# The cached past's key tile among the first token tiles, and the first head's q and k transposed inside the projection stage

## The chip, the cores and the metric

The kernel runs on one core of a Trainium2 chip. The core has five engines that each execute their own list of instructions in order: TensorE (PE), VectorE (DVE), ScalarE (ACT), GpSimd (POOL) and SyncE (SP, which here only issues transfers). The metric is the device time of one execution in microseconds; lower is better.

## The reference

One step of a hybrid encoder layer over 1024 prompt tokens and 64 decode tokens; the decode tokens also see 128 cached positions. What matters here is latent attention with 8 heads: q and kv are projected down to 256 columns, normalised, and projected up; each head's q and k are normalised too.

```python
q = (rmsnorm(c_q, g_cq) @ w_uq).reshape(B, S, N_HEADS, QK_DIM)        # 256 -> 8 x 96
lat_new = rmsnorm(c_kv, g_ckv)                                        # 256 columns
lat_all = lat_new if past_lat is None else jnp.concatenate([past_lat, lat_new], axis=1)
kv = (lat_all @ w_ukv).reshape(B, T, N_HEADS, QK_NOPE + V_DIM)        # 256 -> 8 x (64 + 64)
k_nope = rmsnorm(kv[..., :QK_NOPE], g_kn)
v = kv[..., QK_NOPE:]
```

Ahead of it stands the normalisation and the input projection, behind it softmax over a block-causal mask, the output maps with sigmoid gates, a mixture of 32 experts, and an embedding term. None of that is touched.

## The kernel before

The program runs in stages: the input projection (0 to 282 us of the span), the projections of q and kv from their latents (282 to 407, here called the projection stage), eight heads of attention (407 to 690), the output maps, the router, the experts (897 to 1225) and a tail. A product in f32 is made of two or three matmuls of a high and a low half (`h` and `l` in a tile's name): `mm3` writes them at lines 62 to 64, `mm2` at lines 68 and 69. `hi` casts a high half on ACT (line 56), `lo` takes the rest on DVE (line 59).

The projection stage is a loop over i from 0 to NT + 2, with NT = 9 token tiles. `L_mm(i)` makes the 544 latent columns of tile i on PE (24 matmuls of 256 columns and 24 of 288), `L_stat` and `L_norm` normalise them, `L_tr` transposes them on PE (five transposes), `L_ev` evicts and splits them. Three tiles behind follow `q_a` and `kv_a` (matmuls of 384 and of 512 columns, statistics, and V, which is written to DRAM as `vd`) and `q_b` and `kv_b` (scaling, and writes of q and k to DRAM as `qnd` and `knd`). `qnd` is held in pieces of 4, 4 and 1 tiles, `knd` in pieces of 4, 4 and 2. Tile 9 of k and v belongs to the cached past: its latents come from the input (`pl`), `L_past` splits them, and `kv_a(9)`, `kv_b(9)` make k and v from them, with a `fold` of the two halves by a copy on ACT (line 442) and an add on DVE (line 443). The weights of k and v, `wukv0` and `wukv1`, arrive one after the other through one staging tile, `wup_r`, ahead of the loop, and are split by a cast on ACT and a subtraction on DVE.

From i = NT on, `fill_n(4)` puts gate matmuls (24 of 384 or of 320 columns for a piece) into the stage; they need only `hT` and weights `fw` that POOL's queue loads. All of the stage's PSUM tiles come from `bank()`, a pool of eight. For a head, `kq_load` reloads q and k of two heads into `qs_` and `ks_` on SP's queue (a reload waits for the writes of its piece), `prep_k` and `prep_q` transpose them on PE and split them into kT and qT; S, softmax and PV follow, with more gate matmuls (`fg`) between them.

A scheduler sets the order of each engine's list from the program and its own model; each engine then executes its list strictly in that order, so an instruction that waits holds up all behind it on the same engine. At the end of the stage the code before reads:

```python
    kv_a(9)
    kv_b(9)
    fill_n(4)
    psA.close()
...
    kq_load(0)
    v_load(0)
    v_load(1)
    for f in preps(0):
```

Of the kernel before, what the change touches and what calls it, by code (L numbers as in the profile page):

```python
# [7 lines left out]
F32 = mybir.dt.float32  # L8
# [3 lines left out]
AF = mybir.ActivationFunctionType  # L12
OP = mybir.AluOpType
# [3 lines left out]
T = 1088  # L17
NP = 1024
NS = 64
NT = 9  # L20
# [3 lines left out]
NK = 1216  # L24
# [15 lines left out]
def body(ctx, tc, a):  # L40
    nc = tc.nc
# [9 lines left out]
    def opened(*args, **kw):  # L51
        st = ExitStack()
        return st, st.enter_context(pool(*args, **kw))

    def hi(dst, src):
        nc.scalar.copy(dst, src)  # L56

    def lo(dst, src, h, eng=None):
        (eng or nc.vector).tensor_tensor(out=dst, in0=src, in1=h.bitcast(F32), op=OP.subtract)  # L59

    def mm3(ps, sh, sl, mh, ml, first, last):
        r = nc.tensor.matmul(ps, sh, mh, start=first, stop=False)  # L62
        nc.tensor.matmul(ps, sh, ml, start=False, stop=False)  # L63
        nc.tensor.matmul(ps, sl, mh, start=False, stop=last)  # L64
        return r

    def mm2(ps, st, mh, ml, first, last):
        nc.tensor.matmul(ps, st, mh, start=first, stop=False)  # L68
        nc.tensor.matmul(ps, st, ml, start=False, stop=last)  # L69
# [13 lines left out]
    def rstd(out, ss, scale, n):  # L83
        nc.gpsimd.tensor_scalar(out=out, in0=ss, scalar1=scale, scalar2=EPS, op0=OP.mult, op1=OP.add)
        nc.gpsimd.tensor_tensor(out=out, in0=out, in1=mhalf[:out.shape[0], :n], op=OP.pow)
# [7 lines left out]
    ident = keep.tile([128, 128], F32, name="ident")  # L93
# [16 lines left out]
    def bank():  # L110
        return pb.tile([128, 512], F32, name="bk", tag="bk")
# [249 lines left out]
    for j, (kind, d, g) in enumerate(jobs):  # L361
        if kind == "a" and d == 0:
            open_gate()
        f = evs[kind](d)
# [6 lines left out]
        for ci, (o, n) in enumerate([c for c in CH if c[0] < TB] if kind in "ag" else CH):  # L371
            ps = bank()
# [41 lines left out]
    for src, dst in ((gkr, rk), (gqr, rq)):  # L414
        for half in range(2):
            for w in range(2):
                nc.vector.tensor_tensor(
                    out=dst[:, :, 32 * w + 16 * half:32 * w + 16 * half + 16],
                    in0=rope[:, :, 16 * w:16 * w + 16],
                    in1=src[:, None, 16 * half:16 * half + 16].to_broadcast([128, NT, 16]), op=OP.mult)  # L420
# [20 lines left out]
    def fold(ps, tmp):  # L441
        nc.scalar.copy(tmp[0:64], ps[64:128])
        nc.vector.tensor_tensor(out=ps[0:64], in0=ps[0:64], in1=tmp[0:64], op=OP.add)
# [56 lines left out]
    def L_past():  # L500
        th = lp.tile([128, 2, 128], F32R, name="latTh", bufs=2)
        hi(th[:, :, 0:64], pl[:, :, 64:128])
        lo(th[:, :, 64:128], pl[:, :, 64:128], th[:, :, 0:64])
        latT[9] = (th, None)
# [39 lines left out]
    def kv_a(i):  # L544
        xh, xl = latT.pop(i)
        kn = hwp.tile([128, NH, 64], F32, name="kn")
        V = hwp.tile([128, NH, 128], F32R, name="V", bufs=1)
        p2 = [bank(), bank()]
        for b in range(2):
            for k in range(2):  # L550
                wh, wl = (x[:, 512 * b:512 * b + 512] for x in wk[k])
                if i < 9:
                    mm3(p2[b], xh[:, k], xl[:, k], wh, wl, k == 0, k == 1)
                else:
                    mm2(p2[b], xh[:, k], wh, wl, k == 0, k == 1)
            if i == 9:
                fold(p2[b], kn.rearrange("p h c -> p (h c)"))
        nc.scalar.activation(kn.rearrange("p h c -> p (h c)"), p2[0], AF.Square)
        ss = hwp.tile([128, 8], F32, name="ssk")
        nc.vector.tensor_reduce(out=ss, in_=kn, axis=AX.X, op=OP.add)  # L560
        rs = hwp.tile([128, 8], F32, name="rsk")
        rstd(rs, ss, 1.0 / 64, 8)
        for par in range(2):
            src = p2[1].rearrange("p (j t c) -> p j t c", t=2, c=64)[:, :, par]
            vi = V.rearrange("p (j t) c -> p j t c", t=2)[:, :, par]
            vh = vi[:, :, 64 * par:64 * par + 64]
            hi(vh, src)
            lo(vi[:, :, 64 - 64 * par:128 - 64 * par], src, vh)
        nc.sync.dma_start(vd[:, :, i].rearrange("h p c -> p h c"), V.bitcast(F32))
        st4["k", i] = (p2[0], rs, kn)  # L570

    def kv_b(i):
        p, rs, kn = st4.pop(("k", i))
        nc.vector.tensor_tensor(out=kn, in0=p.rearrange("p (h c) -> p h c", h=8),
                                in1=rs[:, :, None].to_broadcast([128, NH, 64]), op=OP.mult)
        nc.sync.dma_start(knd[i // 4][:, :, i % 4].rearrange("q p c -> p q c"), kn.rearrange("p (q t) c -> p q (t c)", t=2))
# [43 lines left out]
    def fill_n(n):  # L620
        for _ in range(n):
            if fill:
                fill.pop(0)()
# [7 lines left out]
    hws, hwp = opened("hw", bufs=2, side="right")  # L631
    kq, vv = {}, {}

    def kq_load(p):
        qs_ = qk.tile([128, NT, 192], F32, name="qs_", bufs=1)
        ks_ = qk.tile([128, 10, 128], F32, name="ks_", bufs=1)
        for t in range(3):
            k1, q1 = min(10, 4 * t + 4), min(NT, 4 * t + 4)
            nc.sync.dma_start(ks_[:, 4 * t:k1], knd[t][p])
            nc.sync.dma_start(qs_[:, 4 * t:q1], qnd[t][p])  # L640
        kq[p] = (qs_, ks_)

    def v_load(h):
        vv[h] = qk.tile([128, 10, 128], F32R, name="vs_", bufs=2)
        nc.gpsimd.dma_start(vv[h], vd[h])

    for i in range(NT + 3):
        if i < NT:
            L_mm(i)
            L_stat(i)  # L650
        if i == NT - 1:
            gs_["q"].close()
            hs.close()
            fgs, fgp = opened("fgate", bufs=2)
            fg_load(0)
            qks, qk = opened("qk")
            kT = qk.tile([112, 4, NK], F32R, name="kT")
            qT = qk.tile([112, 4, T], F32R, name="qT")
            kTh, kTl, qTh, qTl = ([x[:, s + j] for j in range(2)] for x in (kT, qT) for s in (0, 2))
            qg = qk.tile([96, 1], F32, name="qg")  # L660
            nc.vector.tensor_copy(qg, qgain)
            nc.gpsimd.dma_start(kT[96:112], a["kmask"])
            nc.gpsimd.dma_start(qT[96:112], a["qmask"])
        if 1 <= i <= NT:
            L_norm(i - 1)
        if 2 <= i <= NT + 1:
            L_tr(i - 2)
            L_ev(i - 2)
        if i == NT + 1:
            L_past()  # L670
            for j in range(2):
                nc.scalar.copy(kTh[j][64:96, :], kpe)
                lo(kTl[j][64:96, :], kpe, kTh[j][64:96, :])
        if i >= 3:
            q_a(i - 3)
            kv_a(i - 3)
            q_b(i - 3)
            kv_b(i - 3)
        if i >= NT:
            fill_n(4)  # L680
    kv_a(9)
    kv_b(9)
    fill_n(4)
    psA.close()

# [9 lines left out]
    pT = psS.enter_context(pool("psT", bufs=2, space=PSUM))  # L695
    pO = psS.enter_context(pool("psO", bufs=1, space=PSUM))
    psF.append(psS.enter_context(pool("psF", bufs=1, space=PSUM)))
    def prep_k(h, t0):
        par = h % 2
        kn = kq[h // 2][1]  # L700
        nt = min(4, 10 - t0)
        ps = pT.tile([128, 512], F32, name="tp")
        for t in range(nt):
            nc.tensor.transpose(ps[0:64, 128 * t:128 * t + 128], kn[:, t0 + t, 64 * par:64 * par + 64], ident)
        c = 128 * t0
        n = min(128 * nt, NK - c)
        hi(kTh[par][0:64, c:c + n], ps[0:64, :n])
        lo(kTl[par][0:64, c:c + n], ps[0:64, :n], kTh[par][0:64, c:c + n])

    def prep_q(h, t0):  # L710
        par = h % 2
        qn = kq[h // 2][0]
        nt = min(4, NT - t0)
        ps = pT.tile([128, 512], F32, name="tp")
        for t in range(nt):
            nc.tensor.transpose(ps[0:96, 128 * t:128 * t + 128], qn[:, t0 + t, 96 * par:96 * par + 96], ident)
        c = 128 * t0
        n = min(128 * nt, T - c)
        nc.scalar.activation(qTh[par][0:96, c:c + n], ps[0:96, 0:n], AF.Copy, scale=qg)
        nc.vector.scalar_tensor_tensor(out=qTl[par][0:96, c:c + n], in0=ps[0:96, 0:n], scalar=qg,  # L720
                                       in1=qTh[par][0:96, c:c + n].bitcast(F32), op0=OP.mult, op1=OP.subtract)

    def preps(h):
        return [lambda t0=t0, f=f: f(h, t0) for t0 in (0, 4, 8) for f in (prep_k, prep_q)]

    UN = []
    for h in range(NH):
        for p in (3, 0, 2, 1) if h else (0, 1, 2, 3):
# [100 lines left out]
        nc.vector.tensor_tensor(out=aT[j][g, c0:c0 + n], in0=tmp[g, :n], in1=po[g, :n], op=OP.add)  # L829

    todo = []
    kq_load(0)
    v_load(0)
    v_load(1)
    for f in preps(0):
        f()
# [142 lines left out]
    for d in range(8):  # L979
        w = st6.pop(("w", d))  # L980
        for ci, (o, n) in enumerate(MCH):
            ps = bank()
# [195 lines left out]
    for i in range(6):  # L1178
        p = i - 1
# [345 lines left out]
    with tc.For_i(0, nov, 1) as i:  # L1525
# [7 lines left out]
        ps = bank()  # L1533
# [11 lines left out]
        for k in range(KD):  # L1545
# [4 lines left out]
            h, l = xT["o", k // 4]  # L1550
# [4 lines left out]
        h, l = aT2["o"]  # L1555
        pso = [bank(), bank()]
        for j in range(2):
            for b in range(2):
                c = slice(512 * b, 512 * b + 512)
# [224 lines left out]
```

## Time and profile before

| | |
|---|---|
| time, median of 3 runs | 1350.8 us (1348.19 to 1350.96) |
| profiled execution | 1351.81 us, its span 1349.8 us, mean granted clock 0.982 |
| PE busy | 1268.6 us, 94% of the span |
| DVE, ACT, POOL busy | 848.0, 649.7, 323.8 us |
| PE busy, 400 to 420 us | 14.26 us of 20, granted clock 0.83 |

The times in the rows are microseconds from the start of the span. A row of a timeline gives the start, the duration, the engine, the line of the kernel, the operation, the tile it writes and those it reads, and in brackets the engine's idle time just ahead of it and what ended that. The granted clock is a share of 2.4 GHz. Matmuls overlap in the engine, so the distance of two starts tells more than a duration.

### The profile page before, as it was taken

How to read it: one execution, taken by the hardware profiler on the slowest of the kernel's cores; microseconds unless marked ns; L12 is line 12 of the kernel's file. 1: busy time of each engine (PE TensorE's matmuls, PEld its weight loads, DVE VectorE, ACT ScalarE, POOL GpSimd, SP SyncE). 2: the span in 40 equal slices, each digit the busy share in tenths (PEclk: the TensorE clock that was granted, in tenths of full speed). 3: DMA queues.
4: the chain of work that ended last, by engine and by line, in shares of the span. 5: the costliest groups of instructions: out<-in, count | busy, mean ns of one | idle time of the engine just before them, and what ended most of it. 6: DMA issues, size and time to landing. Idle time of an engine off the chain costs nothing. (4 is left out here: it accounts for less than half of the span.)

```text
span 1349.8 us, 20413 instructions
## 1 busy us (share of the span) xinstructions
PE 1268.6 (94%) x7235; PEld 1100.1 (81%) x7235; DVE 848.0 (63%) x1627; ACT 649.7 (48%) x1276; POOL 323.8 (24%) x375
## 2 busy tenths in 40 slices
PE   7999999998998999999999999749999999999998
PEld 6999999998987988888998888537666666667886
DVE  6433243325675466666659755678988889884743
ACT  6212142223344455555545211338888888886322
POOL 2000001124663333333315200232222222210210
PEclk9999999999998999999999999869999999999999
DMA  5111298734477523242257656769999999967511
GB/s 197 64 34 45 78 355 299 276 117 137 138 188 223 176 69 125 86 150 73 82 197 265 247 201 225 252 185 350 364 346 346 340 345 347 346 235 272 204 39 55
DMA packets 106057, 272.36 MB, mean 202 GB/s; under 512 B 13521, under 2 KB 42689, under 8 KB 105922
## 3 DMA queue, kind: packets, MB, share of 16 engines
q1 hardware_dynamic: 89968, 220.29, 47.1%
q0 software_dynamic: 15840, 50.68, 11.7%
q8 instruction: 58, 0.95, 0.3%
q14 instruction: 45, 0.37, 0.1%
q10 hardware_dynamic: 146, 0.07, 0.0%
HBM read 211.14 MB, written 67.19 MB: 206 GB/s over the span
## 5 line engine op out<-in xcount | busy, mean ns | idle before, releaser
L59 DVE TENSOR_TENSOR wel<-eraw,weh 128x1024 fp32r<-128x1024 f32 x190 | 226.3, 1220 | 34.4 <-ACT weh L56 32.4
L56 ACT CAST weh<-eraw 128x1024 fp32r<-128x1024 f32 x192 | 196.0, 1054 | 11.7 <-PE bk L64 10.7
L769 POOL TENSOR_TENSOR P<-P,ri 128x128 f32<-128x128 f32 (+8 forms) x72 | 77.2, 1077 | 129.2 <-DVE ri L768 109.6
L63 PE MATMUL bk<-wel,xTh 128*96 128x512 f32 x256 | 103.5, 404 | 1.5 <-DVE wel L59 1.4
L62 PE MATMUL bk<-weh,xTh 128*96 128x512 f32 x256 | 102.5, 400 | 1.7 <-ACT xTh L56 1.7
L64 PE MATMUL bk<-weh,xTl 128*96 128x512 f32 x256 | 103.1, 403 | 0.0
L1337 POOL DMA_INDIRECT Yd<-y,idx x32 | 41.3, 1292 | 227.2 <-ACT y L1334 217.5
L59 DVE TENSOR_TENSOR wl<-w_r,wh 128x1024 fp32r<-128x1024 f32 x28 | 34.3, 1225 | 75.7 <-ACT wh L56 75.3
L62 PE MATMUL bk<-hTAh,wh 128*128 128x384 f32 x224 | 76.6, 342 | 1.8 <-ACT hTAh L56 1.8
L63 PE MATMUL bk<-hTAl,wh 128*128 128x384 f32 x224 | 76.4, 341 | 0.0
L64 PE MATMUL bk<-hTAh,wl 128*128 128x384 f32 x224 | 76.1, 340 | 0.0
L62 PE MATMUL fg<-hTBh,fw 128*128 128x384 f32 (+1 forms) x224 | 74.9, 334 | 0.3 <-ACT fgm L605 0.2
L56 ACT CAST wh<-w_r 128x1024 fp32r<-128x1024 f32 x28 | 29.4, 1050 | 91.8 <-PE bk L63 86.3
L64 PE MATMUL fg<-hTBh,fw 128*128 128x384 f32 (+1 forms) x224 | 73.3, 327 | 0.0
L63 PE MATMUL fg<-hTBl,fw 128*128 128x384 f32 (+1 forms) x224 | 73.1, 326 | 0.0
L62 PE MATMUL bk<-hTBh,wh 128*128 128x384 f32 (+1 forms) x192 | 62.2, 324 | 0.0
L63 PE MATMUL bk<-hTBl,wh 128*128 128x384 f32 (+1 forms) x192 | 62.0, 323 | 0.0
L64 PE MATMUL bk<-hTBh,wl 128*128 128x384 f32 (+1 forms) x192 | 61.8, 323 | 0.0
L63 PEld LDWEIGHTS bk<-wel,xTh 128*96 128x96 f32 x256 | 41.7, 163 | 22.2 <-DVE wel L59 7.8
L62 PE MATMUL bk<-weh,ath 128*96 128x512 f32 x128 | 50.9, 397 | 8.8 <-ACT ath L56 8.8
L755 DVE TENSOR_REDUCE nm<-S 128x1 f32<-128x128 f32 (+8 forms) x72 | 50.8, 706 | 12.7 <-PE S L64 11.6
L62 PEld LDWEIGHTS bk<-weh,xTh 128*96 128x96 f32 x256 | 41.6, 162 | 19.3 <-ACT xTh L56 3.3
(782 smaller groups left out, 3750.8 us busy)
## 6 DMA issues: line engine op xcount, KB each, us to landing
eraw<-in_we_dram SPq DMA_DIRECT2D x192, 512.0 KB
fw<-wsd POOLq DMA_DIRECT2D x32, 512.0 KB, 4.3
w_r<-in_wing_dram SPq DMA_DIRECT2D x28, 512.0 KB
gm_r<-gscr SPq DMA_DIRECT2D x16, 544.0 KB
wsd<-wh SPq DMA_DIRECT2D x16, 512.0 KB
wsd<-wl SPq DMA_DIRECT2D x16, 512.0 KB
xy<-Yd SPq DMA_DIRECT2D x16, 512.0 KB
vd<-V SPq DMA_DIRECT2D x10, 512.0 KB
```

What stands on the lines that cost most here:

```text
L56: nc.scalar.copy(dst, src)
L59: (eng or nc.vector).tensor_tensor(out=dst, in0=src, in1=h.bitcast(F32), op=OP.subtract)
L62: r = nc.tensor.matmul(ps, sh, mh, start=first, stop=False)
L63: nc.tensor.matmul(ps, sh, ml, start=False, stop=False)
L64: nc.tensor.matmul(ps, sl, mh, start=False, stop=last)
L755: nc.vector.tensor_reduce(out=nm, in_=s, axis=AX.XY, op=OP.max, negate=True)
L769: nc.gpsimd.tensor_tensor(out=P[:, :nk], in0=P[:, :nk], in1=ri.to_broadcast([128, nk]), op=OP.mult)
L1337: nc.gpsimd.indirect_dma_start(out=Yd[:, :], out_offset=bass.IndirectOffsetOnAxis(ap=col, axis=0), in_=buf, in_offset=None, bounds_check=A ...
```

## The change

`L_past()`, `kv_a(9)` and `kv_b(9)` move from the end of the loop to i = 2. `kq_load` takes a range of pieces; for the first two heads its first two pieces are put at i = NT + 1 and its third at i = NT + 2. `prep_k` and `prep_q` move up in the program and can take a bank of the stage's pool; for head 0 the first two pieces of both are transposed at i = NT + 2, ahead of the last gate fill, and `preps(0)` keeps only the third piece.

```diff
@@ -631,18 +631,46 @@
-    def kq_load(p):
-        qs_ = qk.tile([128, NT, 192], F32, name="qs_", bufs=1)
-        ks_ = qk.tile([128, 10, 128], F32, name="ks_", bufs=1)
-        for t in range(3):
+    def kq_load(p, ta=0, tb=3):
+        if ta == 0:
+            kq[p] = (qk.tile([128, NT, 192], F32, name="qs_", bufs=1), qk.tile([128, 10, 128], F32, name="ks_", bufs=1))
+        qs_, ks_ = kq[p]
+        for t in range(ta, tb):
             k1, q1 = min(10, 4 * t + 4), min(NT, 4 * t + 4)
             nc.sync.dma_start(ks_[:, 4 * t:k1], knd[t][p])
             nc.sync.dma_start(qs_[:, 4 * t:q1], qnd[t][p])
-        kq[p] = (qs_, ks_)
...
+    def prep_k(h, t0, get=None):
+        par = h % 2
+        kn = kq[h // 2][1]
+        nt = min(4, 10 - t0)
+        ps = get() if get else pT.tile([128, 512], F32, name="tp")
+        for t in range(nt):
+            nc.tensor.transpose(ps[0:64, 128 * t:128 * t + 128], kn[:, t0 + t, 64 * par:64 * par + 64], ident)
...
+    def preps(h):
+        return [lambda t0=t0, f=f: f(h, t0) for t0 in ((0, 4, 8) if h else (8,)) for f in (prep_k, prep_q)]
...
@@ -661,13 +689,16 @@
+        if i == 2:
+            L_past()
+            kv_a(9)
+            kv_b(9)
         if 1 <= i <= NT:
             L_norm(i - 1)
         if 2 <= i <= NT + 1:
             L_tr(i - 2)
             L_ev(i - 2)
         if i == NT + 1:
-            L_past()
             for j in range(2):
...
@@ -676,10 +707,15 @@
+        if i == NT + 1:
+            kq_load(0, 0, 2)
         if i >= NT:
             fill_n(4)
-    kv_a(9)
-    kv_b(9)
+        if i == NT + 2:
+            kq_load(0, 2, 3)
+            for t0 in (0, 4):
+                prep_k(0, t0, bank)
+                prep_q(0, t0, bank)
     fill_n(4)
     psA.close()
...
-    kq_load(0)
     v_load(0)
```

Where this puts instructions on PE, among the first tiles (`wukv` is the weight of k and v, `latTh` the past's latents, `ident` marks a transpose of `L_tr`, `wq` the matmuls of `L_mm`); lines with a plus are new there:

```order
 L64 MATMUL bk<-wq7h,hTAl 128x288
+L68 MATMUL bk<-wukv0h,latTh 128x512 x2
 L479 MATMUL bk<-ident,cq 128x128
 L480 MATMUL bk<-ident,ltk 128x128
...
 L63 MATMUL bk<-wq4l,hTBh 128x288
+L68 MATMUL bk<-wukv1h,latTh 128x512 x2
 L64 MATMUL bk<-wq4h,hTBl 128x288
...
 L64 MATMUL bk<-wq7h,hTBl 128x288
+L69 MATMUL bk<-wukv1l,latTh 128x512 x2
 L479 MATMUL bk<-ident,cq 128x128
```

The eight matmuls of the past's tile now stand in four pairs: the first behind `L_mm(2)`, one within `L_mm(3)` (not shown), one ten matmuls before the end of `L_mm(3)`, and one behind it.

PE at the end of the stage, before: behind the gate fill of 384 columns stand the matmuls of the past's tile, and only behind the fill of 320 columns the first transposes of q and k (`ks_`, `qs_`):

```order
L68 MATMUL bk<-wukv0h,latTh 128x512
...
L69 MATMUL bk<-wukv1l,latTh 128x512
L62 MATMUL bk<-hTBh,fw_3722 128x320
...
L64 MATMUL bk<-hTBh,fw_3723 128x320
L704 MATMUL tp<-ident,ks__4045 64x128 x4
L716 MATMUL tp<-ident,qs__4044 96x128 x4
L704 MATMUL tp<-ident,ks__4045 64x128 x4
L62 MATMUL S<-kT,qT 128x128
L63 MATMUL S<-kT,qT 128x128
```

and of the change:

```order
L64 MATMUL bk<-hTBh,fw_3755 128x384
L653 MATMUL bk<-ident,ks__3860 64x128 x4
L665 MATMUL bk<-ident,qs__3859 96x128 x4
L653 MATMUL bk<-ident,ks__3860 64x128 x4
L665 MATMUL bk<-ident,qs__3859 96x128 x4
L62 MATMUL bk<-hTBh,fw_3754 128x320
...
L64 MATMUL bk<-hTBh,fw_3755 128x320
L653 MATMUL tp<-ident,ks__3860 64x128 x2
L665 MATMUL tp<-ident,qs__3859 96x128
L62 MATMUL S<-kT,qT 128x128
L63 MATMUL S<-kT,qT 128x128
```

Two pieces of k and of q stand ahead of the fill of 320 columns, and the first S stands behind the third piece of both.

SP at the same place, before (`knd` and `qnd` are the pieces in DRAM, `kn` and `qn` what is written to them, `gscr` and `fy` belong to the gates):

```order
L640 DMA qs__4044<-qnd_65 128x768
L576 DMA knd_69<-kn 128x4x128
L611 DMA gscr<-fgm 128x384
L594 DMA fy<-ycd 128x320
L639 DMA ks__4045<-knd_68 128x512
L542 DMA qnd_66<-qn 128x4x192
L611 DMA gscr<-fgm 128x320
L594 DMA fy<-ycd 128x384
L569 DMA vd<-V 128x8x128
L576 DMA knd_69<-kn 128x4x128
L640 DMA qs__4044<-qnd_66 128x192
L639 DMA ks__4045<-knd_69 128x256
```

and of the change:

```order
L641 DMA qs__3859<-qnd_65 128x768
L576 DMA knd_69<-kn 128x4x128
L640 DMA ks__3860<-knd_68 128x512
L611 DMA gscr<-fgm 128x384
L594 DMA fy<-ycd 128x320
L640 DMA ks__3860<-knd_69 128x256
L542 DMA qnd_66<-qn 128x4x192
L641 DMA qs__3859<-qnd_66 128x192
```

The reload of the second piece of k moves ahead of the gates' transfers, that of the third piece ahead of the last q write, and the past's writes are gone from here.

## Rows read from the trace of the kernel before

**Rows 1.** Windows: busy time of each engine by stretch, clock, DMA share, GB/s.

```profile
core 0: us, PE busy (x) PEld busy (x) DVE busy (x) ACT busy (x) POOL busy (x), PEclk, DMA share, GB/s
320.00:400.00 80.00, 78.72 (x497) 74.04 (x496) 57.21 (x163) 31.64 (x100) 47.65 (x57) 1.00 0.52 144
400.00:420.00 20.00, 14.26 (x73) 13.26 (x72) 10.97 (x26) 5.24 (x11) 9.75 (x12) 0.83 0.96 295
430.00:690.00 260.00, 250.36 (x1696) 234.96 (x1695) 161.34 (x359) 140.85 (x361) 90.98 (x97) 1.00 0.34 109
```

**Rows 2.** Timeline of PE, 299 to 319: start, duration, line, operation, [idle before].

```profile
300.34 0.27 PE L479 MATMUL bk<-ident,cq 128*128 128x128 f32 x1
...
306.87 0.27 PE L479 MATMUL bk<-ident,cq 128*128 128x128 f32 x1
...
307.33 0.42 PE L62 MATMUL bk<-wuq0h,cqTh 128*128 128x384 f32 x1
...
313.83 0.72 PE L62 MATMUL bk<-wukv0h,latTh 128*128 128x512 f32 x1 [4.17 <-ACT qn L520]
...
318.26 0.28 PE L62 MATMUL bk<-wq0h,hTBh 128*128 128x256 f32 x1
```

**Rows 3.** Timeline of ACT, 298 to 320: the casts of the wukv weights.

```profile
300.96 1.05 ACT L56 CAST wukv0h<-wup_r 128x1024 fp32r<-128x1024 f32 x1 [4.72 <-DMA wup_r<-in_wukv_dram]
...
310.99 1.04 ACT L56 CAST wukv1h<-wup_r 128x1024 fp32r<-128x1024 f32 x1 [6.98 <-DMA wup_r<-in_wukv_dram]
```

**Rows 4.** Timeline of PE, 397 to 424: end of the projection stage, first head.

```profile
397.49 0.33 PE L62 MATMUL bk<-hTBh,fw 128*128 128x384 f32 x1
...
401.65 0.40 PE L68 MATMUL bk<-wukv0h,latTh 128*128 128x512 f32 x1
...
403.50 0.31 PE L62 MATMUL bk<-hTBh,fw 128*128 128x320 f32 x1
...
407.02 0.60 PE L704 MATMUL tp<-ident,ks__4045 128*64 128x128 f32 x4
...
413.97 1.06 PE L704 MATMUL tp<-ident,ks__4045 128*64 128x128 f32 x4 [4.81 <-DVE kT L59]
...
415.15 0.63 PE L62 MATMUL fg<-hTBh,fw 128*128 128x384 f32 x1
...
421.84 0.33 PE L64 MATMUL fg<-hTBh,fw 128*128 128x384 f32 x1
...
422.25 0.38 PE L704 MATMUL tp<-ident,ks__4045 128*64 128x128 f32 x2
...
423.39 0.44 PE L62 MATMUL S<-kT,qT 112*128 112x384 f32 x1 [0.63 <-ACT P L762]
```

**Rows 5.** Timeline of ACT, 399 to 420: first fold copy of the past's tile.

```profile
406.09 0.58 ACT L442 COPY kn<-bk 64x512 f32<-64x512 f32 x1 [3.75 <-DMA knd<-kn]
```

**Rows 6.** Timeline of DVE, 399 to 420: rest of the first k block.

```profile
413.24 0.67 DVE L59 TENSOR_TENSOR kT<-tp,kT 64x512 fp32r<-64x512 f32 x1
```

**Rows 7.** Timeline of POOL, 395 to 420: the last q tile's rsq.

```profile
402.76 2.90 POOL L90 TENSOR_TENSOR rsq<-rsq,mhalf 128x16 f32<-128x16 f32 x1
```

**Rows 8.** Timeline of SP, 395 to 420: issues of writes and reloads.

```profile
401.04 0.36 SPq L542 DMA_DIRECT2D qnd<-qn  x1
...
401.64 0.36 SPq L576 DMA_DIRECT2D knd<-kn  x1
...
403.80 0.33 SPq L640 DMA_DIRECT2D qs__4044<-qnd  x1
...
404.22 1.29 SPq L576 DMA_DIRECT2D knd<-kn  x1
...
410.82 0.37 SPq L542 DMA_DIRECT2D qnd<-qn  x1
...
415.68 0.33 SPq L640 DMA_DIRECT2D qs__4044<-qnd  x1
...
418.83 0.33 SPq L639 DMA_DIRECT2D ks__4045<-knd  x1
```

**Rows 9.** DMA issues, 395 to 425: KB each, median us to landing.

```profile
fw<-wsd POOLq DMA_DIRECT2D x4, 512.0 KB, 4.8
```

More of the change, by code (lines that the diff above doesn't have):

```diff
@@ L645, in v_load, with prep_q @@
         nc.gpsimd.dma_start(vv[h], vd[h])
+    def prep_k(h, t0, get=None):
[5 more added lines that the diff above has]
+            nc.tensor.transpose(ps[0:64, 128 * t:128 * t + 128], kn[:, t0 + t, 64 * par:64 * par + 64], ident)
+        c = 128 * t0
+        n = min(128 * nt, NK - c)
+        hi(kTh[par][0:64, c:c + n], ps[0:64, :n])
+        lo(kTl[par][0:64, c:c + n], ps[0:64, :n], kTh[par][0:64, c:c + n])
+    def prep_q(h, t0, get=None):
+        par = h % 2
+        qn = kq[h // 2][0]
+        nt = min(4, NT - t0)
+        ps = get() if get else pT.tile([128, 512], F32, name="tp")
+        for t in range(nt):
+            nc.tensor.transpose(ps[0:96, 128 * t:128 * t + 128], qn[:, t0 + t, 96 * par:96 * par + 96], ident)
+        c = 128 * t0
+        n = min(128 * nt, T - c)
+        nc.scalar.activation(qTh[par][0:96, c:c + n], ps[0:96, 0:n], AF.Copy, scale=qg)
+        nc.vector.scalar_tensor_tensor(out=qTl[par][0:96, c:c + n], in0=ps[0:96, 0:n], scalar=qg,
+                                       in1=qTh[par][0:96, c:c + n].bitcast(F32), op0=OP.mult, op1=OP.subtract)
+    def preps(h):
+        return [lambda t0=t0, f=f: f(h, t0) for t0 in ((0, 4, 8) if h else (8,)) for f in (prep_k, prep_q)]
     for i in range(NT + 3):
@@ L697, in body @@
     psF.append(psS.enter_context(pool("psF", bufs=1, space=PSUM)))
[L698 to L724, printed above, removed]
     UN = []
```

## The prediction

> **What bounds the kernel now.** I read the engines' busy shares by stretch first, then the timeline of PE around the two places that the diff touches, then the timelines of ACT, DVE, POOL and SP there, to see what ends PE's waits. PE sets the pace: from 320 to 400 us it is busy 78.72 of 80, and in the heads, from 430 to 690, 250.36 of 260 [rows 1]. An instruction put on PE there, or a wait of PE there, is therefore paid nearly in full. Between those two stretches lies the one visible hole: from 400 to 420 PE works 14.26 us of 20 and its granted clock is 0.83 [rows 1]. A second one lies at the start of the stage: PE stands 4.17 us before the matmul at 313.83 [rows 2]. The change works at both places.
>
> How the late hole comes about: the eight matmuls of the cached past's tile (I call them kv9) run from 401.65 to 403.50, the gate fill of 320 columns to 407.02, then the first four k transposes; the next k transposes start only at 413.97, after a wait that DVE's kT ended [rows 4]. That kT (413.24, [rows 6]) needs ACT's cast, and ACT came late because the fold copy of kv9 waited 3.75 us for the write of an older kn and began at 406.09 [rows 5]; all of kv9's copies and casts stood ahead of kT on ACT. After the wait the fill of 24 matmuls takes from 415.15 until its last one starts at 421.84, so 6.86 us to its end at about 422.0, against 4.16 for the same 24 from 397.49 to 401.65 [rows 4]: 2.7 us lost at the lower of the two clock levels (1.2 instead of 2.4 GHz). Wait and slow clock together are about 8.5 us, which the change aims at.
>
> **The early place.** kv9's matmuls now stand in the first token tiles, in four pairs. The first pair needs wukv0h, whose cast runs from 300.96 to 302.01 [rows 3]; PE gets there at 300.34 [rows 2] and so waits 1.7. L_tr(0) and L_mm(3) take 6.53 (300.34 to 306.87, [rows 2]); the third pair stands ten matmuls before their end, ten of 48 being some 1.3 us. A matmul of 512 columns costs 1.85 / 8 = 0.23 [rows 4]. So PE has 2 x 0.46 + 5.2 to do and is at the third pair at 302.0 + 6.1 = 308.2, but wukv1h is cast only from 310.99 to 312.03, when its weights have landed [rows 3]: a wait of 3.9. Those weights come by a transfer issued long before; nothing in the change moves it. What is left behind this wait: the third pair 0.46, ten matmuls 1.3, the fourth pair 0.46, L_tr(1) 0.46 (306.87 to 307.33), q_a(0) some 2.2 (from 307.33, with the 4.17 of idle before 313.83 taken off), and the twelve matmuls of kv_a(0), 12 x 0.23 = 2.8 [rows 2]. That is 7.7, to 319.7, against 318.26 before: +1.4 with a full clock throughout. Before, kv_a(0) after its wait of 4.17 took 4.43 (313.83 to 318.26) instead of 2.8, 1.65 lost to the lower clock [rows 2]. A wait of 3.9, with one of 1.7 just ahead, is nearest to that row, so I add 1.65: +3.1. If the clock stays low as long as in the late row, 2.7 instead of 1.65: +4.1. The range of this term is +1.4 to +4.1. The old wait of 4.17 is not a saving: it was the same wait for wukv1h, with ACT's work behind it, and it is now met with more work left over. kv9's own 1.85 is inside this term, since PE has no other idle time until 400.
>
> Also moved with it: the fold, square and casts on ACT and DVE and the writes of vd and knd on SP. In tile 0 ACT has idle time and PE has L_mm(4), some 6 us, to run meanwhile; I cost them at nothing, and take their exposure as a rival.
>
> **The late place**, in the clock time of the trace before, PE at 401.65 [rows 4]. kv9 is gone, so the first k and q transposes follow at once, 0.4 each (five took 0.46 at 306.87, [rows 2]): PE is done at 402.5. Next on PE, in front of the fill, stand the second k transposes, and they need the reload of the second key block. On SP this reload stands behind the knd write at 404.22, which took 1.29 to issue, and needs the write issued at 401.64 to be back [rows 8]. A write is back 2.8 (401.04 to 403.80) to 4.9 later (410.82 to 415.68) [rows 8]. So the issue falls at 405.5 to 406.5. The trace before shows no duration for this read. The reload issued at 418.83 was used at 422.25, so it took 3.4 at most [rows 4, 8]; 512 KB loads take 4.8 [rows 9]; I use 2.8 to 4.8, taking the shortest write as the floor. The block of 256 KB is then there at 408.3 to 411.3, and I take 409.8. **PE waits 7.3** (5.8 to 8.8), and the fill of 3.5 us (403.50 to 407.02) that covered such waits before is now queued behind the waiting transposes. Then k and q transposes 0.9, the fill 3.5 and, after a wait as long as that of 413.97, the same 2.7 of slow clock: 416.9 (415.4 to 418.4).
>
> Behind it on PE stand the last k and q transposes, which need the reload of the last q block. Its chain: the q write stands on SP behind the reload of the last k block, and that one waits for the knd write of 404.22 to come back, 407.0 to 409.1. Its data need rsq, which POOL has at 405.66 [rows 7], and seven short DVE operations, ready earlier than before, when the fold stood among them and the write was issued at 410.82 [rows 8]. So the issue is at 407.4 to 410.8; I take 409.0. With a write of 2.8 to 4.9 and a read of 2.8 to 4.8 the block lands at 413 to 420.5, middle 416.7. Both legs end together; S starts at about 417.4, three S matmuls take 0.4, the fill of 24 at full clock 4.16: 421.9, against 422.0 for the same point before. What before still had behind that point is saved: the last k transposes, 0.14 (422.25), and a wait of 0.63 in front of 423.39 [rows 4], since softmax starts earlier. **Late term: -0.9** (-2.5 to +2.6, from the ends of both chains).
>
> So the hole of 8.5 is not closed: kv9's tail is replaced by the way through DRAM and back, and the fill that hid part of that way now stands behind it.
>
> Here a rule can be set against the rows. What the rows show is 2.8 to 4.9 for one leg [rows 8]. The Trainium skill, "DMA: Bandwidth & Descriptors", section "Anatomy of one DMA", puts a transfer at some 2.0 us fixed plus the bytes over the rate. By it, as an estimate, the reload of 256 KB would take 2.6 and the write as long, and the sum would be that of the first rival. The rows of this stretch stand above it, with DMA busy 0.96 of the time [rows 1], so I go by them.
>
> **Sum.** +3.1 - 0.9 = +2.2 us. On the profiled execution (1351.81, its span 1349.8) that is 1354.0; it stands 1.0 over the median of the runs, so on 1350.8 I forecast **1353.0**. A measurement of this kernel can tell about 0.2% from no change, 2.7 us, and the forecast lies just within.
>
> **Rivals.**
> 1. Short legs: every write and read takes 2.8. Then the second key block lands at 408.3, PE is through the fill at 415.4 and the last q block lands at 413.0: late -2.5. With the early term at its middle the sum is +0.6, 1351.4. For it: the leg of 2.8 at 401.04. Against: the leg of 4.9 nine us later. Chance 0.2.
> 2. Faster, by the clock alone: PE keeps 2.4 GHz over both waits. Early +1.4; late, with 2.7 less in front of S, 416.9 becomes 414.2, but S still waits for the last q block, so this counts only if that one lands by then: late -0.9 - 3.2 = -4.1. Sum -2.7, 1348.1; the point that decides is S started by 414.2 with fill matmuls at 0.15 to 0.17 us each. Against it speak both waits of before, after each of which the clock fell. Chance 0.15 with versions still better.
> 3. Slower, early: V has one buffer, so V of tile 0 waits for the write of kv9's V, and ACT stands in order behind it. A write of 4.9 [rows 8] after the first cast, with ACT's queue behind it, would hold up q_a(1) and the banks; beyond the 6 us of L_mm(4) that cover it I see 2 to 4 us at worst. Sum +5 to +6, about 1356. Chance 0.15.
> The forecast has 0.5, its own range being +0.5 to +4.5.
>
> **Numbers.** The range takes in rival 1 whole, most of rival 2's mild side and rival 3: 1348.5 to 1358. Slower by over 0.2% comes from nearly half of the forecast's case and from rival 3: 0.43; faster from rival 2 and a little of rival 1: 0.17; within: 0.40.
>
> **What would show it.** In the profile after: PE idle of about 1.7 before a wukv0h pair near 300 and of 3 to 4 before a wukv1h pair, released by ACT, with the 256-column matmul that began at 318.26 now 1.4 to 4.1 later; in the late place PE idle of 6 to 9 before the second k transposes, released by a DMA, with fill matmuls near 0.27 behind it, and the first S some 2.5 to 3 later than 414.68 relative to the 384-column fill at 397.49. The prediction is wrong if the reload is there when PE comes, if the clock does not fall, or if PE finds a new wait between 320 and 400.

## The result, and the profile after

The changed kernel takes 1361.38 us (median of 4 runs, 1361.18 to 1365.45) against 1350.2 before: 1.0088 of the time before, with an interval of 1.0073 to 1.0104, so 11.2 us slower. I had forecast 1353.0 with a range of 1348.5 to 1358. A second series of the same kernel gave 1363.42 us, 1.0115 (1.0098 to 1.0132). The profiled execution is the one of 1365.45 us, 4 us above the other three; so I compare single stretches, each from its own mark, and not the totals.

The early place in the changed kernel, timeline of PE:

```profile
300.29 0.73 PE L68 MATMUL bk<-wukv0h,latTh 128*128 128x512 f32 x2 [1.84 <-ACT wukv0h L56]
...
310.22 1.12 PE L68 MATMUL bk<-wukv1h,latTh 128*128 128x512 f32 x2 [3.48 <-ACT wukv1h L56]
...
319.57 0.28 PE L62 MATMUL bk<-wq0h,hTBh 128*128 128x256 f32 x1
```

The two waits stand where they were forecast, 1.84 (1.7) and 3.48 (3.9). PE came to the first at 300.29 - 1.84 = 298.45, before at 300.34 [rows 2]; from there to the first matmul of the next `L_mm` it takes 21.12 us, before 17.92. The early term is +3.2, forecast +3.1. At the fill of 384 columns it is (399.25 - 298.45) - (397.49 - 300.34) = +3.65. In the profiled execution of the second series the two waits are 2.43 and 2.14, and the term is +2.5, at the fill +2.7.

The late place, timeline of PE:

```profile
399.25 0.33 PE L62 MATMUL bk<-hTBh,fw 128*128 128x384 f32 x1
...
411.60 1.04 PE L653 MATMUL bk<-ident,ks__3860 128*64 128x128 f32 x4 [7.15 <-DMA ks__3860<-knd]
...
413.14 0.61 PE L62 MATMUL bk<-hTBh,fw 128*128 128x320 f32 x1
...
418.43 0.38 PE L653 MATMUL tp<-ident,ks__3860 128*64 128x128 f32 x2 [0.15 <-DMA ks__3860<-knd]
424.11 0.45 PE L665 MATMUL tp<-ident,qs__3859 128*96 128x128 f32 x1 [5.30 <-DMA qs__3859<-qnd]
...
424.89 0.63 PE L62 MATMUL fg<-hTBh,fw 128*128 128x384 f32 x1
...
431.25 0.33 PE L64 MATMUL fg<-hTBh,fw 128*128 128x384 f32 x1
...
431.77 0.34 PE L62 MATMUL S<-kT,qT 112*128 112x384 f32 x1
```

From the fill at 399.25 to the first S of 384 columns at 431.77 it is 32.5 us, before 25.9 [rows 4]: +6.6 (+6.8 in the second series), where I had -0.9. The first half came as forecast: the wait for the second k piece is 7.15 (7.3), and the fill of 320 columns is done 19.0 us after 399.25 (19.4 after 397.49). Then PE waits 5.30 more for the last q block, and the 24 fill matmuls behind that run slowly again: 424.89 to 431.42, 6.5 us instead of 4.16. The windows show both clock drops, a granted clock of 0.83 in either half:

```profile
core 0: us, PE busy (x) PEld busy (x) DVE busy (x) ACT busy (x) POOL busy (x), PEclk, DMA share, GB/s
400.00:420.00 20.00, 11.50 (x63) 10.57 (x61) 10.73 (x26) 4.36 (x9) 9.44 (x11) 0.83 0.90 273
420.00:440.00 20.00, 15.89 (x86) 15.65 (x87) 5.54 (x16) 7.08 (x17) 3.59 (x6) 0.83 0.35 110
```

Some of the loss lies further back, in the heads. PE's first matmul of the output maps, in the kernel before and in the changed one:

```profile
693.46 0.44 PE L62 MATMUL bk<-aTh,woah 128*128 128x384 f32 x1 [2.29 <-ACT woah L56]
704.16 0.45 PE L62 MATMUL bk<-aTh,woah 128*128 128x384 f32 x1 [1.98 <-ACT woah L56]
```

Without that idle time, PE is through the heads 293.7 us after the start of the fill of 384 columns before, and 302.9 in the changed kernel (301.6 in the second series): +9.3 (+7.9), of which 6.6 (6.8) are there at the first S of 384.

The timeline of SP shows where the last q block was:

```profile
406.01 1.14 SPq L576 DMA_DIRECT2D knd<-kn  x1
407.20 0.63 SPq L640 DMA_DIRECT2D ks__3860<-knd  x1
...
410.82 0.32 SPq L640 DMA_DIRECT2D ks__3860<-knd  x1
411.18 0.43 SPq L542 DMA_DIRECT2D qnd<-qn  x1
419.72 0.32 SPq L641 DMA_DIRECT2D qs__3859<-qnd  x1
```

The q write is issued at 411.18, 11.9 us after the fill's start (11.5 in the forecast), and the reload that waits for it goes out at 419.72: the write took 8.5 us, where I had 3.9 with 4.9 as the upper end. The k reload of 128 KB issued just ahead of it, at 410.82, is in use only at 418.43. On POOL's queue the two V loads of 640 KB each had gone out just before:

```profile
409.26 0.62 POOL L645 DMA_DIRECT2D vs__4080<-vd  x1 [1.80 <-issue]
409.89 0.54 POOL L645 DMA_DIRECT2D vs__4082<-vd  x1
418.43 1.06 POOL L586 DMA_DIRECT2D fw<-wsd  x2 [8.00 <-PE bk L64]
```

Before, these two stood behind the gate weights on POOL and waited for the write of the past's V:

```profile
407.33 1.17 POOL L586 DMA_DIRECT2D fw<-wsd  x2 [1.67 <-PE bk L64]
...
418.64 0.60 POOL L645 DMA_DIRECT2D vs__4052<-vd  x1 [6.04 <-DMA vd<-V]
```

Now they are free to go, since the past's V is written early, and the gate weights wait for the fill that PE holds back.

### The profile page after: what moved, and what is told of

It is laid out like the page before. It is cut to its first block, busy times and chain, and to the rows that moved or that the text cites. A ratio compares the mean times of both kernels' runs of the same rounds, so it can differ in the third digit from the quotient of the medians.

```text
span 1363.3 us, 20406 instructions
## 1 busy us (share of the span) xinstructions
PE 1272.7 (93%) x7235; PEld 1102.5 (81%) x7235; DVE 849.8 (62%) x1627; ACT 650.3 (48%) x1276; POOL 326.3 (24%) x375
## 5 line engine op out<-in xcount | busy, mean ns | idle before, releaser
L56 ACT CAST weh<-eraw 128x1024 fp32r<-128x1024 f32 x192 | 195.9, 1054 | 11.9 <-PE bk L64 11.8
L1344 POOL DMA_INDIRECT Yd<-y,idx x32 | 43.0, 1344 | 225.4 <-ACT y L1341 214.5
L763 DVE TENSOR_REDUCE nm<-S 128x1 f32<-128x128 f32 (+8 forms) x72 | 50.8, 706 | 19.4 <-PE S L64 18.1
L59 DVE TENSOR_TENSOR PlA<-tp,PhA 128x512 fp32r<-128x512 f32 (+1 forms) x66 | 38.1, 589 | 30.5 <-ACT PhA L56 30.4
```

The source lines that it names most:

```text
L763: nc.vector.tensor_reduce(out=nm, in_=s, axis=AX.XY, op=OP.max, negate=True)
L1344: nc.gpsimd.indirect_dma_start(out=Yd[:, :], out_offset=bass.IndirectOffsetOnAxis(ap=col, axis=0), in_=buf, in_offset=None, bounds_check=A ...
```

## Experiments

Theory A: the loss lies in the late place. The reloads lost their cover, and the bulk loads issued just ahead of them lengthen the last write and reloads. Theory B: the early place bears most of it. All ratios are to the kernel before on the same chip.

**Each half alone.** The first takes only the past's tile to i = 2, the second only the reloads and transposes up:

```diff
@@ first: the kernel before
+        if i == 2:
+            L_past()
+            kv_a(9)
+            kv_b(9)
...
-            L_past()
...
-    kv_a(9)
-    kv_b(9)
@@ second: the changed kernel
-        if i == 2:
-            L_past()
-            kv_a(9)
-            kv_b(9)
...
+            L_past()
...
         if i == NT + 2:
+            kv_a(9)
+            kv_b(9)
             kq_load(0, 2, 3)
```

> Only the past's tile moves to i = 2; reloads and first transposes stay as before. Theory A (the loss lies in the late place: reloads stand ahead of the fill that covered them, and the last q write and k reload are slowed by the V loads beside them): early cost about +3.8 as in the changed kernel, but the late hole of 8.5 us closes because the past's tail is gone and fills cover the reloads: 1344 to 1350 us. Theory B (the early place costs most of the 11 us, by waits that spread through the stage): 1355 us or more.

> Only the reloads and first transposes move up; the past's tile stays at the end of the stage, and the first S no longer stands behind the third pieces. Theory A: no early loss; PE waits some 6 us for the second k piece with the fill behind it, and the clock falls once: within 2 us of before, 1349 to 1353 us. Rival (putting the reloads ahead of the fill costs the 7 us by itself): 1356 us or more.

Measured: the past's tile early 1349.77 us (0.9989, 0.9978 to 1.0001); the transposes early 1356.93 (1.0048, 1.0035 to 1.0061). So B is out for the tile by itself: with fills left between the reloads and their use, its early cost is paid back late (in its trace +2.0 up to the fill of 384 columns, -6.9 from there to the end of the heads). For the second run A's number missed and its rival's held. Its trace shows a wait of 2.1 us for the third k piece, whose reload was issued at 418.37, straight behind 1 MB of gate weights and the two V loads; I had not expected that mechanism there. Ahead of the second k transposes PE waits 5.5 us, but not for the reload alone:

```profile
410.10 1.03 PE L653 MATMUL bk<-ident,ks__3831 128*64 128x128 f32 x4 [5.46 <-ACT V L56]
```

The row puts the end of the wait down to ACT's cast of the past's V, out of a bank of the same pool; the reload, issued at 405.52 and 4.4 us on the way, landed at about the same time. The two halves come to -1.1 and +6.1, so 5.0 of the 11 to 13 us; the other 6 to 8 appear only when both are there. (In the second run the first S also no longer stands behind the third pieces, so it isn't the changed kernel less the tile to the last instruction.)

**The V loads.** The changed kernel, with `v_load(0)` and `v_load(1)` made to wait for the last q transposes of head 0:

```diff
-        nc.gpsimd.dma_start(vv[h], vd[h])
+        r = nc.gpsimd.dma_start(vv[h], vd[h])
+        if late:
+            tc.add_manual_dep(r.ins, late[-1].name, ...)
...
```

> The changed kernel, with the first two V loads made to wait for the last q transposes of head 0 (so that they start behind the last reload). Theory A: the last q write and k reload take 3 to 5 us instead of 7.5 to 8.5, the wait of 5.3 us in front of the last q transposes shrinks to 0 to 1.5 and the low clock behind it goes: 1354 to 1356 us. Rival (the two transfers are slow by themselves or by the queue they stand in): waits as in the changed kernel, 1360 to 1362 us.

Measured: 1356.07 us (1.0046, 1.0033 to 1.0059), 5 to 7 us less than the changed kernel. Timelines of SP and of POOL:

```profile
410.57 0.32 SPq L640 DMA_DIRECT2D ks__3860<-knd  x1
410.94 0.43 SPq L542 DMA_DIRECT2D qnd<-qn  x1
414.09 0.32 SPq L641 DMA_DIRECT2D qs__3859<-qnd  x1
```

```profile
417.65 1.17 POOL L586 DMA_DIRECT2D fw<-wsd  x2 [10.40 <-PE bk L64]
418.82 0.53 POOL L645 DMA_DIRECT2D vs__4089<-vd  x1
```

The same write now takes 414.09 - 410.94 = 3.15 us, since nothing bulky is under way (gate weights and V go out only from 417.65). PE's wait of 5.30 is gone, the one of 7.1 stays. The Trainium skill, "DMA: Bandwidth & Descriptors", section "Anatomy of one DMA", gives for GpSimd's path 2.0 us and the bytes over the rate, for these 384 KB, as an estimate, 2.9: this write on SyncE's queue agrees with nothing bulky under way (3.15), and beside 1.3 MB of other loads it doesn't (8.5).

**The cover.** The changed kernel, with only the first pieces transposed ahead of the fill of 320 columns:

```diff
-        return [lambda t0=t0, f=f: f(h, t0) for t0 in ((0, 4, 8) if h else (8,)) for f in (prep_k, prep_q)]
+        return [lambda t0=t0, f=f: f(h, t0) for t0 in ((0, 4, 8) if h else (4, 8)) for f in (prep_k, prep_q)]
...
-            for t0 in (0, 4):
+            for t0 in (0,):
                 prep_k(0, t0, bank)
                 prep_q(0, t0, bank)
```

> The changed kernel, but only the first k and q pieces are transposed ahead of the fill of 320 columns; the second pieces go behind it, as the third ones. Theory A: the fill and the first S cover the reload, the wait of 7.2 us and the one of 5.3 shrink to under 2 together, the early cost of 3.8 stays: 1344 to 1349 us. Rival (the reloads come so late that PE waits anyway, only further back): 1356 us or more.

Measured: 1354.77 us (1.0034, 1.0021 to 1.0047), 7 to 9 us less than the changed kernel, but 6 above the upper end that A gave. The wait of 7.2 is gone; one of 3.3 for the third k piece takes its place, since V still goes out at 409.90 ahead of its reload, and gate weights too. The q write here takes 11.2 us:

```profile
411.94 0.43 SPq L542 DMA_DIRECT2D qnd<-qn  x1
...
423.12 0.32 SPq L641 DMA_DIRECT2D qs__3859<-qnd  x1
```

**Where the tile goes.** i = 5 instead of 2, when both weights are there: in the changed kernel, and alone. Then alone with V late; and in the changed kernel with V late and the second pieces behind the fill.

```diff
-        if i == 2:
+        if i == 5:
```

> The changed kernel with the past's tile at i = 5 instead of 2, when both weights have long been split; the late place as in the changed kernel. Theory (the early cost is the wait for wukv1 with more work left behind it, about 2 us beyond the tile's own 1.85): some 2 us less than the changed kernel, 1358 to 1360 us, PE waiting once near 310 as before. Rival (the early position costs little, all is late): 1361 us.

> The kernel before with only the past's tile moved, to i = 5; reloads and transposes as before. Against the run with it at i = 2 (1349.8 us): theory 1 to 2 us less, 1347.5 to 1349; the V loads, which move ahead with it, still slow the second k reload by 2 to 3 us. Rival (early position without effect): 1349.8.

> As the past's tile at i = 5 alone, with the first two V loads behind the second q transposes of head 0. Theory: the last reloads take 2 to 4 us instead of 6 to 9, the wait for the second k piece (2.5 us with the tile at i = 2) goes: 1 to 3 us less than without the delay, 1345 to 1347 us. Rival (V then comes late for the first PV): no gain or a new wait of PE for V.

> All three repairs at once: the past's tile at i = 5, the second pieces behind the fill, the first two V loads behind the second q transposes. Theory: the early cost falls to the tile's own 1.85 us, taken from the late place, the late waits fall under 2 us together and the clock stays up: 4 to 7 us faster than before, 1344 to 1347 us. Rival (the time is given back in the heads): 1350 us.

Measured: 1364.28 (1.0097, 1.0076 to 1.0117), 1348.49 (0.9983, 0.9971 to 0.9996), 1353.64 (1.0020, 1.0007 to 1.0033) and 1350.52 (0.9987, 0.9974 to 1.0000). The first missed; beside the second series of the changed kernel (1363.4, single runs from 1360.3 to 1368.2) it tells nothing. The second came out as expected. The fourth missed its 1344 to 1347: a wait of 2.1 us for the third k piece is left, whose reload (412.26) again has gate weights (409.23) ahead of it. The third missed the other way: with V held back the time rose by 5. Its timelines of POOL and SP say why:

```profile
408.21 1.17 POOL L586 DMA_DIRECT2D fw<-wsd  x2
419.58 0.53 POOL L645 DMA_DIRECT2D vs__4089<-vd  x1 [10.21 <-PE S L64]
```

```profile
409.85 2.59 SPq L639 DMA_DIRECT2D ks__4045<-knd  x2
412.49 0.43 SPq L542 DMA_DIRECT2D qnd<-qn  x1
...
418.33 0.32 SPq L640 DMA_DIRECT2D qs__4044<-qnd  x1
```

The next pair of gate weights, also 1 MB, went out at 408.21, ahead of the k reloads at 409.85 to 412.4; in the run without the delay V went out first at 410.25, behind the first of these reloads (409.56). PE got the second k piece at 417.08, after a wait of 3.7 that was 0.2 there.

**Gate weights held too.** I put the same wait on the fourth pair of gate weights, in two runs:

> The run with the past's tile at i = 5 and V late, and now the fourth pair of gate weights (1 MB, which had taken V's place ahead of the reload) held behind the second q transposes as well. Theory (any 1 MB load issued shortly ahead of a reload lengthens it, whichever it is): the second k reload takes about 4 us and the third one 2 to 3, PE's wait of 3.7 us and the low clock behind it go: 1345 to 1348 us. Rival (holding loads back costs the fills their weights): a new wait of PE for fw near 424, 1350 us or more.

> The run with the three repairs (1350.5 us), and the fourth pair of gate weights held too. Theory: its one wait of 2.1 us for the third k piece and the low clock behind it go: 1346 to 1348.5 us. Rival: no change, 1350.5.

They gave 1353.15 us (1.0026) and 1349.77 (0.9990), but tell nothing on the theory: the wait was set before the program had made that load, so the load still went out at 407.25 and 408.3. In earnest, on the kernel with the tile at i = 5 and V late:

```diff
+                if j == 3:
+                    tc.add_manual_dep(r.ins, held[-1].name, ...)
```

> The run with the past's tile at i = 5 and V late (1353.6 us), and the fourth pair of gate weights really behind the second q transposes, after V. Theory (whichever bulk load is issued ahead of the reloads lengthens them): the second k reload takes about 4 us instead of 7 to 8, PE's wait of 3.7 to 4.4 us in front of it goes with the low clock, 1346 to 1349 us unless the gate weights then come late for the third fill of the heads (another wait of PE near 430). Rival (the reload is slow for another reason): wait and time unchanged, 1353.

Measured: 1348.53 us (0.9979, 0.9967 to 0.9992), 5 less. Timelines of POOL and SP:

```profile
415.94 0.62 POOL L649 DMA_DIRECT2D vs__4089<-vd  x1 [6.93 <-DMA qnd<-qn]
...
417.10 1.37 POOL L586 DMA_DIRECT2D fw<-wsd  x2
```

```profile
410.17 2.80 SPq L643 DMA_DIRECT2D ks__4045<-knd  x2
413.02 0.43 SPq L542 DMA_DIRECT2D qnd<-qn  x1
...
416.37 0.32 SPq L644 DMA_DIRECT2D qs__4044<-qnd  x1
```

Now both bulk loads stand behind the q write; that takes 3.35 us, and PE's wait for the second k piece is 0.3.

**The early wait by itself.** A second buffer for the staging tile, so that wukv1 is loaded while wukv0 is split: in the run that meant to hold both loads, in the one with the tile at i = 5, in the changed kernel and in the kernel before.

```diff
-            r = up.tile([128, 1024], F32, name="wup_r", tag="wup_r", bufs=1)
+            r = up.tile([128, 1024], F32, name="wup_r", tag="wup_r", bufs=2)
```

> As the run that holds both loads, and the staging tile of the up-projection weights has two buffers, so that wukv1 is loaded while wukv0 is split. Theory (the early wait is for these weights alone): PE's wait of some 4 us near 310 shrinks to under 1.5 and the clock stays up there: 3 to 5 us less than without, 1341 to 1344 us. Rival (the two loads then share the queues and end no earlier): the same time.

> The past's tile at i = 5 alone (1348.5 us), and two buffers for the staging tile of the up-projection weights. Theory: the wait of 4 us near 310 and the low clock behind it go, as they did with the V load delayed (1353.4 to 1346.9 us): 1341 to 1344 us. Rival: the late place gives part of it back, 1345 to 1347.

> The changed kernel with two staging buffers: the weights of both pairs are there early, so both early waits (1.8 and 3.5 us) go, and the late place is as in the changed kernel. Theory (early term about 3 to 4 us with the tile's own 1.85, late about 7 to 8): the early waits and their low clock are worth 5 to 7 us, 1355 to 1358 us, late waits of 7 and 5 us unchanged. Rival (the early place bears most of the loss): 1352 or less.

> The kernel before with two staging buffers and nothing else: its wait of 4.17 us at 313.83 and the low clock behind it (1.65) go, the late hole stays: 1344 to 1347 us. Rival (the second load takes as long beside the first): 1350.

> The changed kernel once more, beside the others: 1361 to 1364 us, both late waits of 7 and 5 us in its trace, as before.

Measured: 1346.88 (0.9974, 0.9962 to 0.9985), 1344.44 (0.9953, 0.9936 to 0.9970), 1354.25 (1.0026, 1.0013 to 1.0039) and 1344.65 (0.9951, 0.9934 to 0.9968); the changed kernel beside the first of these 1363.42. PE's waits from 296 to 430 us, in the changed kernel and in the kernel before, each with two buffers (what it waited for, us in total, times, longest):

```profile
PE bk L653 <- DMA ks__3860<-knd: 7.4, 1, 7.4
PE tp L665 <- DMA qs__3859<-qnd: 4.2, 1, 4.2
PE tp L653 <- DMA ks__3860<-knd: 1.4, 1, 1.4
```

```profile
PE tp L704 <- DVE kT L59: 4.8, 1, 4.8
PE bk L62 <- issue: 1.6, 1, 1.6
PE tp L716 <- ACT kn L442: 0.9, 1, 0.9
```

The early waits are gone in both. Without them the change costs 1354.25 - 1344.65 = 9.6 us. The kernel before gains 5.9 by it, the changed one 7 to 9: so the waits of the early place hold some 1 to 3 us of the 11. In their traces 1.6 of the 9.6 comes up to the fill of 384 columns (about the tile's own 1.85, which only moved here from the late place) and 7.6 from there to the end of the heads.

**Both places repaired.** The tile at i = 5, V and the gate weights held, two buffers: first with the transposes left where they were before, then with the first pieces ahead of the fill and the others behind it.

> The past's tile at i = 5, V and the fourth pair of gate weights behind the second q transposes, two staging buffers. Theory (both places repaired, effects add): the run with both held (1348.5 us) less the 4 to 6 us that two staging buffers gave elsewhere: 1342 to 1344.5 us. Rival (with the early waits gone, what is left late is bounded by the same reloads as in the kernel before with two staging buffers): 1344.5, no gain over that one.

> The run with the three repairs (first pieces transposed before the fill, the others behind it, V late), gate weights held in earnest, two staging buffers. Theory: 1349.8 us less 4 to 6 us: 1344 to 1346 us; PE's wait of 1.6 to 2.1 us for the third k piece goes, 1342 to 1344.5. Rival: transposing the first pieces within the stage gains nothing over leaving them behind the fill, 1344.5 or more.

Measured: 1342.22 us (0.9940, 0.9923 to 0.9958) and **1339.42 us (0.9920, 0.9898 to 0.9942)**, the latter 11 to 12 us faster than before and the lowest of all. For the first the gains add up; the second came out below both of its ranges, and why it gains more is not shown. The intervals of the two overlap; in their traces PE is through the heads 286.1 and 283.8 us after the start of the fill of 384 columns (293.7 before). Windows of the last one:

```profile
core 0: us, PE busy (x) PEld busy (x) DVE busy (x) ACT busy (x) POOL busy (x), PEclk, DMA share, GB/s
300.00:320.00 20.00, 20.00 (x146) 19.46 (x145) 11.38 (x38) 7.27 (x32) 10.21 (x17) 1.00 0.51 164
400.00:440.00 40.00, 38.76 (x252) 37.01 (x251) 22.26 (x52) 18.14 (x42) 15.38 (x18) 1.00 0.69 221
```

PE works 38.76 of 40 us at full clock where the kernel before had its hole (there 33.63, at 0.91).

## Why the prediction was wrong

The direction of the sum was right, its size far off, and the step that failed is one term. In the early place the waits and what releases them were right: 1.84 and 3.48 us, and +3.2 where I had +3.1. That the sum fits so well is in part luck, since the 1.65 in it for the low clock does not always come: with the tile at i = 2 alone, the waits are 1.78 and 3.53, the clock stays at 1.00, and the term is +1.7, near the +1.4 that I had for a full clock; the five traces that share this place give +1.1 to +3.2. The first half of the late term was right: the wait for the second k piece, the slow fill behind it, and even the issue of the last q write, within 0.4 us.

**The step "the last q block lands at 413 to 420.5, middle 416.7" failed.** It lands 24.9 us after the fill's start, where the middle was 19.2 and the upper end 23.0. Of these 5.7 us, 0.4 lie in the issue, 0.6 in the reload (419.72 to 424.11) and 4.7 in the write. This leg was mis-sized: 8.5 us, taken as 2.8 to 4.9 from rows of a stretch in which V loads did not yet run [rows 8]. In the changed kernel V stands ahead of the gate weights on POOL's queue; I named the past's writes that go and costed nothing for what comes in. That the V loads make the 8.5 is shown: with them held back the write takes 3.15 in the changed kernel. With a pair of gate weights ahead of it and V held back it takes 5.8 (412.49 to 418.33). The 5.3 of wait cost 2.4 more by the clock; the first S came 25.0 after the fill's start instead of 19.9, and those 5.1 with the 2.4 make the 7.5 between -0.9 and +6.6. The part of the loss that lies in the heads had no term at all.

One reading was off, at little cost. The 6.86 us that I gave to 24 fill matmuls [rows 4] also hold four q transposes and a matmul of S (420.24 to 420.74), so the low clock cost 2.2 there and not 2.7.

Of the rivals, the short legs of 2.8 came true only with the bulk loads held back (2.8 to 3.35), and then not as a part of this change. The second rival did not come: the clock fell behind the early wait of 3.48 and behind each late wait. The third, V's single buffer, did not show: PE's only new wait there is 0.5 us at 327.82. What the change aims at was right, and the fastest kernel keeps half of it: the first pieces are transposed within the stage, while fills cover the way through DRAM of the others.

Open stays what costs 2.6 us (1.1 in the second series) in the heads behind the first S of 384. Open is also why the tile at i = 2 alone gains only 1.1 in the median, though its profiled execution, the second shortest of its series, is 4.8 us shorter (1347.04 against 1351.81). A single execution is no measure of such differences: from the first matmul of the output maps to the end, which no edit here touches, the profiled executions take 655.9 to 662.2 us.

## What to carry to other kernels

Loads that were set free by something moved ahead lengthened the small writes and reloads issued behind it, though they stood on another engine's queue: look at what else becomes ready, and hold bulk loads behind the transfers that the critical engine waits for. Work that covers a wait has to stand ahead of the waiting instruction in the engine's list; ahead of its cover, an early instruction only waits earlier. Before work is pulled to a place, ask what that place already waits for: here a second staging buffer was worth 6 us in the kernel before, more than the move of the tile by itself (1.1 and 2.4).

## What the runs showed of the hardware that I had not expected

Two loads of 640 KB on GpSimd's queue made a write of 384 KB on SyncE's queue take 8.5 us instead of 3.15; the queues did not shield one from the other. All the profiled executions fit this. From the issue of this write to that of the reload that waits for it they show 2.8 to 3.4 us in the five where no bulk load was issued in the 5 us ahead of it, 4.9 to 6.5 in the seven with 1 MB of gate weights 3 to 4.5 us ahead, and 8.2 to 11.2 in the eight with both V loads some 2 us ahead.

And the same wait does not always cost the clock. With the past's tile at i = 2 alone, PE waited early as long as in the changed kernel:

```profile
301.63 0.73 PE L68 MATMUL bk<-wukv0h,latTh 128*128 128x512 f32 x2 [1.78 <-ACT wukv0h L56]
...
311.60 0.73 PE L68 MATMUL bk<-wukv1h,latTh 128*128 128x512 f32 x2 [3.53 <-ACT wukv1h L56]
```

It waited 2.5 us late, too, yet the granted clock stayed at 1.00, 2.4 GHz, over both stretches (first two rows); in the changed kernel, over the same early stretch, it was 0.94 (last row):

```profile
core 0: us, PE busy (x) PEld busy (x) DVE busy (x) ACT busy (x) POOL busy (x), PEclk, DMA share, GB/s
296.00:325.00 29.00, 23.69 (x165) 22.12 (x164) 14.01 (x39) 9.10 (x28) 10.62 (x19) 1.00 0.44 145
400.00:425.00 25.00, 21.57 (x139) 20.66 (x138) 13.71 (x38) 9.20 (x22) 12.77 (x16) 1.00 0.97 310
296.00:325.00 29.00, 23.68 (x153) 21.98 (x152) 13.77 (x37) 9.11 (x28) 9.63 (x17) 0.94 0.42 143
```

With V late in the changed kernel, waits of 1.89 and 1.42 us in this place left it at 0.94; with only the first pieces ahead of the fill, waits of 1.58 and 3.22 left it at 1.00. What decides between the two is open.
